# Two-layer attention block: wide score maxima, value sums in a score bank and later scaling in layer 0; an early shared rotary tile and a halved last gate slice in layer 1

## The chip, the cores and the metric

The kernel runs on 1 core of one Trainium2 chip. The metric is the device time of one execution in microseconds. The kernel before took 1701.79 us (median of 3 runs, 1701.4 to 1703.03).

## The reference

Two layers act on 1024 latent tokens and 256 context tokens, each 1024 wide, in float32. In each layer the tokens are normalised and modulated, projected to queries, keys, values and a gate, go through softmax attention, are multiplied by silu(gate) and projected back:

```python
y = (o * silu(g)) @ w_out          # per layer
x = x + gate * y
# layer 0: 16 query heads of width 64, 4 key/value heads; latent queries read 1024 latent + 256 context keys,
#          context queries read the 256 context keys only
# layer 1: 16 heads; score = q_nope . k_nope (64 wide) + q_rope . k_rope (32 wide, one rotary key for all heads);
#          only latent queries
p = softmax(scale * q k^T);  o = p v
```

The result is the latent stream after both layers.

## The kernel before, in words

Products need float32 accuracy, so an operand is split into a high and a low part and a product is three matmuls: high x high, high x low, low x high.

**Attention** (class `Attention`, one object per layer) walks over units. A latent unit of layer 0 is one head with its 1024 queries; a context unit is the four heads of one key group with 4 x 256 queries. Layer 0 has 20 units in the order of `units`: latent heads 0 to 3, a context unit, heads 4 to 7, a context unit, heads 8 to 15, two context units. Layer 1 has 16 latent units. `run` (L640 onwards) goes through them: for each key tile of 128 keys (10 in a latent unit, 2 in a context unit of layer 0) `scores_by_halves` (L486) computes a score tile `st` of 128 keys by 1024 queries in two PSUM banks. The contraction is only 64 wide, so queries 0 to 511 work in rows 0 to 63 of the array and queries 512 to 1023 in rows 64 to 127, side by side: four pairs of matmuls in layer 0 (three products, and one that subtracts the query's maximum), five in layer 1. ScalarE takes the exp (L508) into `p`. After all key tiles of a unit follow, in this order:

- `run_turns`: for a unit whose maxima are complete, TensorE turns the 128x8 maxima (L422), VectorE casts them into `crow` (one buffer, L424), and two loads carry them into the row that the last score product subtracts (`shift`, a tile per unit in flight; `minus` holds the -1 that selects the row);
- `add_up`: GpSimd adds up the exp tiles (`acp`, L542), helped by VectorE for the last four (`pair_sum`, `acd`, L528);
- `totals` of the unit before: TensorE sums over the keys (L597) into a maxima bank, VectorE turns it and takes the reciprocal; `later` sets when the rows are spread (4 steps on), the output scaled by them on GpSimd (6) and stored (9);
- `do_av`: the value sums (L555) into the bank `av`, then ScalarE copies them out (L576) in `finish`.

The maxima of units ahead are computed between the scores (`max_parts`, L385): a half step is 128 queries by 512 keys in one PSUM bank `mx`, one matmul, and one reduction on VectorE (L395; L404 for context keys). Two half steps go with each key tile, one for each half of the array; `lead` says how many were done before the first unit, in layer 0 among the last gate slices (four at a time).

**PSUM** has eight banks. In layer 0's attention: three for `mx`, four for two score tiles, one for `av`.

**Order.** In `run` the instructions of TensorE, VectorE and ScalarE are issued in the order written; GpSimd and the load queue SP, and all engines in the gate slices and projections around it, are ordered by a planner. Each engine works in its order.

**Layer 1's start.** The last score product of layer 1 reads the shared tile `KS`: the rotary key and a row of -1, for all heads. It is opened in `l1_open_late` with the late tiles, in memory that the hidden state `hT` has until the last gate slice (L1728).

Of the kernel before, what the change touches and what calls it, by code (L numbers as in the profile page):

```python
# [19 lines left out]
P = 128  # L20
D = 1024
KT = D // P
# [6 lines left out]
HALVES = (True, True)  # L29

# [6 lines left out]
def hybrid_kernel(ctx: ExitStack, tc: tile.TileContext, ins: dict, out: bass.AP):  # L37
# [271 lines left out]
    class Attention:  # L309
# [15 lines left out]
        def open_early(self, st):  # L325

            l = self.l
            self.kp = st.enter_context(tc.tile_pool(name=f"kp{l}", bufs=self.ops["kbufs"], side="right", reuse_waits="tile"))
            self.qp = st.enter_context(tc.tile_pool(name=f"qp{l}", bufs=self.ops["qbufs"], side="right", reuse_waits="tile"))
            self.ps_m = st.enter_context(tc.tile_pool(name=f"psm{l}", bufs=3 if HALVES[l] else 2, space=PSUM, side="right", reuse_waits="tile"))  # L330
            if HALVES[l]:
                self.ops["open"](self, st)

        def open_late(self, st, stp):
            l = self.l
            self.op = st.enter_context(tc.tile_pool(name=f"op{l}", bufs=3 - l, reuse_waits="tile"))
            if l and HALVES[l]:
                self.ops["open_late"](self, stp)
# [71 lines left out]

        def do_shift(self, u):
# [8 lines left out]
            def turn():  # L420
                t = self.ps_m.tile([P, 512], F32, name="mx", tag="mx")[:8, :P]
# [11 lines left out]
        def start_unit(self):  # L433
# [3 lines left out]
            s["m"] = self.sm.tile([P, 8, 3 if lat else 1], F32, name="m", tag="m" if lat else "mc")  # L437
# [3 lines left out]
            if HALVES[self.l]:  # L441
# [9 lines left out]
        def next_maxima(self, upto, limit):  # L451

            steps = []
            while self.done < upto:
# [5 lines left out]
                self.done += 1  # L460
                half, parts = self.max_parts(u, m)
# [30 lines left out]
        def scores_by_halves(self, u, kt, p, steps):  # L492
# [11 lines left out]
            for half, parts in steps:  # L504
                at_ = (last + 2) // 2 if half and self.l else 0
# [25 lines left out]
        def add_up(self, u, parts, last):  # L531
# [3 lines left out]
            for b in parts:  # L535
# [5 lines left out]
                t = self.ap.tile([P, 1024], F32, name="acp", tag="acp", bufs=2) if len(held) == 2 else a  # L541
# [4 lines left out]
        def do_av(self, u, group, ps):  # L546
# [3 lines left out]
            if group[0] == kts[0]:  # L550
                s["av"] = self.ps_o.tile([P, 512], F32, name="av", tag="av")
# [19 lines left out]
        def finish(self, u):  # L571
# [21 lines left out]
            def total():  # L593
                t = s["av"] if u is not self.units[-1] and not HALVES[l] else self.ps_m.tile([P, 512], F32, name="mx", tag="mx")
# [9 lines left out]
                self.later((4, spread), (6, scale), (9, store))  # L604
# [24 lines left out]
        def run(self, lead, ahead, extra, tail):  # L629
# [3 lines left out]
            with tc.manual_schedule(engines={mybir.EngineType.PE, mybir.EngineType.DVE, mybir.EngineType.Activation}):  # L633
                for t, u in enumerate(self.units):
# [13 lines left out]
                    for group in (kts[:cut], kts[cut:]):  # L648
# [21 lines left out]
                        if final:  # L670
                            tail()
                        self.run_turns()
# [7 lines left out]
                        while self.totals:  # L680
                            self.totals.pop(0)()
# [5 lines left out]
                        self.step += (2 + len(group)) // 3  # L687
                while self.totals:
                    self.totals.pop(0)()
# [520 lines left out]
    def l0_open(at, st):  # L1210
        pool_ = st.enter_context(tc.tile_pool(name="shift0", bufs=1, **right))
        at.minus = pool_.tile([P, P], F32R, name="minus")
        at.shift = [pool_.tile([P, 512], F32R, name=f"shift{i}") for i in range(4)]
        for t in (at.minus, *at.shift):
            pool.memset(raw(t), 0.0)
        for n in range(2):
            pool.memset(raw(at.minus[64 * n:64 * n + 1, :]), -1.0)

    def l0_load_halves(u, at, lat, KH, KL):
# [3 lines left out]
        QH = qp.tile([P, 512], F32R, name="QH", tag="QA")  # L1223
        QL = qp.tile([P, 512], F32R, name="QL", tag="QB")
        for t, src in ((QH, q0h), (QL, q0l)):
            for n in range(2):
                dst = raw(t[64 * n:64 * n + 64, :])
                if lat:
                    h = u["h"]
                    sp.dma_start(dst, src[h // 2, 64 * (h % 2):64 * (h % 2) + 64, 512 * n:512 * n + 512])  # L1230
                else:
                    sp.dma_start(dst.rearrange("p (a n) -> p a n", a=2),
                                 src[2 * g:2 * g + 2, 64 * n:64 * n + 64, NL:].rearrange("a p n -> p a n"))
        X = at.shift[i]
        return dict(KH=KH, KL=KL, QH=QH, QL=QL, X=X, minus=at.minus, crow=[X[64 * n:64 * n + 1, :] for n in range(2)])
# [42 lines left out]
    def l0_maxima(s, n):  # L1278
        r = slice(64 * n, 64 * n + 64)
        return [(s["QH"][r, :], s["KH"][r, :])]  # L1280

    def l0_scores(s, kt, n=None):
        ks = slice(kt * P, (kt + 1) * P)
        if n is not None:
            r = slice(64 * n, 64 * n + 64)
            return [(s["KH"][r, ks], s["QH"][r, :]), (s["KL"][r, ks], s["QH"][r, :]),
# [16 lines left out]
    at = Attention(0, units, dict(scale=0.125, load=l0_load, scores=l0_scores, maxima=l0_maxima, mparts=1, open=l0_open, kbufs=2, qbufs=3, vw=256))  # L1303
# [21 lines left out]
    wo.append(load_weight(ins["l0_w_out"], KT, 512, 512, 0, todo=pieces))  # L1325
# [3 lines left out]
    at.run(28, 3, pieces, lambda: first.extend(fetch_first(0, 2)))  # L1329
# [269 lines left out]
    at = Attention(1, units, dict(scale=float(96 ** -0.5), load=l1_load, scores=l1_scores, maxima=l1_maxima, mparts=2, open=l1_open, open_late=l1_open_late,  # L1599
# [201 lines left out]
```

## Time and profile before

| | |
|---|---|
| median of 3 runs | 1701.79 us |
| the profiled execution | 1701.99 us, its span 1700.2 us |
| granted TensorE clock, mean | 0.996 |
| attention of layer 0, first score to last totals | 372.25 to 748.8 us |
| attention of layer 1, first score to last totals | 1189.42 to 1608 us |
| busy: TensorE / VectorE / ScalarE / GpSimd | 1659.7 / 1040.8 / 641.7 / 959.9 us |

Times in the views are microseconds from the start of the span. PE is TensorE's matmuls, PEld its weight loads, DVE VectorE, ACT ScalarE, POOL GpSimd, SP the load queue. In a line of the order of time stand start, duration, engine, line, operation, output<-inputs, shape and count; in brackets the idle time before it and what ended it. A line of stretches has the stretch, its length, the busy time of PE, PEld, DVE, ACT and POOL (with counts), then the granted TensorE clock (1.00 is full), the share of DMA engines busy and GB/s. A line of waits has who waited for whom: total, times, longest.

### The profile page before, as it was taken

The page shows a single profiled execution, that of the slowest core. Times are in us where ns is not written, and L with a number is a line of the kernel's source. Part 1 is how long each engine was busy: PE and PEld are TensorE (multiplying, and loading weights), DVE is VectorE, ACT ScalarE, POOL GpSimd, SP SyncE. Part 2 cuts the span into 40 slices and gives each one's busy share as a digit, 9 for nine tenths or more (in the row PEclk, how much of TensorE's full clock was granted, in tenths as well). Part 3 has the DMA queues.
Part 4 walks back from the last instruction along what each step waited for, and adds up shares of the span by engine and source line. Part 5 has one row for each costly group of instructions (what it writes and reads, how often), then busy time and mean ns, then how long its engine had stood idle before and what let it go on. Part 6 is the DMA issues. An engine that isn't in the chain of part 4 may idle for free. (4 is left out here: it accounts for less than half of the span.)

```text
span 1700.2 us, 27393 instructions
## 1 busy us (share of the span) xinstructions
PE 1659.7 (98%) x10212; PEld 1210.6 (71%) x10212; DVE 1040.8 (61%) x1807; ACT 641.7 (38%) x943; POOL 959.9 (56%) x646
## 2 busy tenths in 40 slices
PE   8999999999999999999989999999999999999998
PEld 5776768776566666557878889886766667667587
DVE  3765552357788777625675657754778777777231
ACT  4642212124455544432244533330434434344310
POOL 2673441218789988843245554450668787787521
PEclk9999999999999999999999999999999999999999
DMA  9547854521242422156433866776565555653451
GB/s 313 170 147 241 260 165 153 155 81 45 63 123 60 112 63 63 39 140 201 140 94 116 232 193 183 217 205 149 128 144 136 132 120 121 143 127 89 122 166 73
DMA packets 219821, 238.97 MB, mean 141 GB/s; under 512 B 23016, under 2 KB 159192, under 8 KB 219688
## 3 DMA queue, kind: packets, MB, share of 16 engines
q1 hardware_dynamic: 219264, 237.11, 50.0%
q8 instruction: 81, 1.33, 0.3%
q14 instruction: 52, 0.43, 0.1%
q10 hardware_dynamic: 424, 0.11, 0.0%
HBM read 163.37 MB, written 73.63 MB: 139 GB/s over the span
## 5 line engine op out<-in xcount | busy, mean ns | idle before, releaser
L395 DVE TENSOR_REDUCE m<-mx 128x1 f32<-128x512 f32 x512 | 333.5, 687 | 177.8 <-PE mx L393 174.2
L508 ACT ACTIVATE p<-st 128x1024 f32<-128x1024 f32 x328 | 335.9, 1027 | 164.2 <-PE st L501 144.1
L542 POOL TENSOR_TENSOR acp<-acp,p 128x1024 f32<-128x1024 f32 x128 | 305.3, 2385 | 7.8
L555 PE MATMUL av<-p,v 128*64 128x512 f32 x1312 | 291.2, 597 | 0.0
L555 PEld LDWEIGHTS av<-p,v 128*64 128x64 f32 x1312 | 91.1, 137 | 181.6 <-issue 179.0
L542 POOL TENSOR_TENSOR acp<-p 128x1024 f32<-128x1024 f32 x34 | 81.4, 2395 | 147.6 <-ACT p L508 147.5
L542 POOL TENSOR_TENSOR acp<-acp,acd 128x1024 f32<-128x1024 f32 x60 | 141.9, 2364 | 20.9 <-DVE acd L528 17.8
L528 DVE TENSOR_REDUCE acd<-p 128x512 f32<-128x1024 f32 x124 | 144.6, 1220 | 7.9 <-ACT p L508 7.8
L136 POOL TENSOR_TENSOR wb<-wraw,wa 128x512 fp32r<-128x512 f32 (+3 forms) x73 | 95.4, 1325 | 78.7 <-ACT wa L157 78.7
L93 PE MATMUL mm<-wa,hh 128*128 128x512 f32 (+2 forms) x336 | 127.5, 379 | 2.0 <-ACT hh L890 2.0
L501 PE MATMUL st<-QH,KH 64*128 64x512 f32 x320 | 122.6, 406 | 1.0 <-DVE gth L303 1.0
L95 PE MATMUL mm<-wa,hl 128*128 128x512 f32 (+2 forms) x336 | 121.5, 362 | 1.4 <-DVE hl L893 1.3
L94 PE MATMUL mm<-wb,hh 128*128 128x512 f32 (+2 forms) x336 | 121.0, 360 | 0.0
L501 PE MATMUL st<-QH,KL 64*128 64x512 f32 x320 | 119.4, 395 | 0.0
L576 ACT COPY os<-av 128x512 f32<-128x512 f32 x36 | 21.1, 587 | 260.2 <-PE av L555 206.8
L501 PE MATMUL st<-QL,KH 64*128 64x512 f32 x320 | 118.7, 392 | 0.0
L93 PE MATMUL y<-wa,oh 128*128 128x512 f32 (+1 forms) x296 | 114.1, 386 | 0.0
L95 PE MATMUL y<-wa,ol 128*128 128x512 f32 (+1 forms) x296 | 113.5, 383 | 0.0
L94 PE MATMUL y<-wb,oh 128*128 128x512 f32 (+1 forms) x296 | 113.5, 383 | 0.0
L404 DVE TENSOR_REDUCE m<-mx 128x2 f32<-128x512 f32 x144 | 94.2, 688 | 22.2 <-PE mx L403 18.8
L393 PE MATMUL mx<-KH,QH 64*128 64x512 f32 x256 | 102.8, 407 | 0.3 <-DVE m L404 0.3
L93 PE MATMUL mm<-hh,wa 128*128 128x512 f32 x256 | 101.9, 398 | 0.6 <-DVE qt L1675 0.6
(240 smaller groups left out, 3940.1 us busy)
## 6 DMA issues: line engine op xcount, KB each, us to landing
mraw<-in_l_w_mod SPq DMA_DIRECT2D x64, 256.0 KB
wraw<-in_l_w_in SPq DMA_DIRECT2D x28, 512.0 KB
KH<-k1h SPq DMA_DIRECT2D x32, 320.0 KB
KL<-k1l SPq DMA_DIRECT2D x32, 320.0 KB
rb<-rrow SPq DMA_DIRECT2D x72, 128.0 KB
mraw<-in_l_w_mod SPq DMA_DIRECT2D x16, 512.0 KB
sgd<-gth SPq DMA_DIRECT2D x32, 256.0 KB
wraw<-in_l_w_out SPq DMA_DIRECT2D x16, 512.0 KB
```

The lines of the kernel that those rows point to most:

```text
L93: pe.matmul(ps, lhsT=lh(k), rhs=rh(k), start=first and i == 0, stop=False)
L94: pe.matmul(ps, lhsT=lh(k), rhs=rl(k), start=False, stop=False)
L95: pe.matmul(ps, lhsT=ll(k), rhs=rh(k), start=False, stop=last and i == len(ks) - 1)
L136: eng.tensor_sub(lo, a, b)
L393: pe.matmul(held["m"][:, cs], lhsT=q[:, t * P:(t + 1) * P], rhs=k[:, ks], start=j == 0, stop=j == len(pairs) - 1)
L395: dve.reduce_max(s["m"][:, i, n:n + 1], held["m"], axis=AX.X)
L404: dve.reduce_max(s["m"][:, 2 * i:2 * i + 2, 2 if u["kind"] == "lat" else 0], m.rearrange("p (a b) -> p a b", a=2), axis=AX.X)
L501: pe.matmul(ps[:, n * 512:(n + 1) * 512], lhsT=lh, rhs=rh, start=j == 0, stop=j == last)
L508: act.activation(p, ps, AF.Exp, scale=self.ops["scale"])
L528: dve.reduce_sum(t[:, ns], p2.rearrange("p a n -> p n a")[:, ns, :], axis=AX.X)
L542: pool.tensor_add(t, a, b)
L555: pe.matmul(s["av"][64 * n:64 * n + 64, :], lhsT=s["v"][:, kt, u["vc"]:u["vc"] + 64], rhs=p[:, n * 512:(n + 1) * 512], start=kt == kts[0], ...
```

## The change

Layer 0:
- A maxima step is wide: 128 queries against all 1024 latent keys (keys 0 to 511 in rows 0 to 63, 512 to 1023 in rows 64 to 127), into a two-bank tile and with one reduction of 1024. For that all 1024 queries (`QA`) are loaded into both halves of the rows. Two such buffers take four banks. One wide step goes with each key tile; two at a time and at most 14 in all among the gate slices.
- The bank `av` is gone. The value sums go into a buffer of the score tiles, or, once no maxima are left to do, into a maxima buffer.
- Totals are no longer made in a context unit (but for the last two units); where two are made together, the second's later steps are three further on. Spreading, scaling and storing come 4, 8 and 11 steps on. `acp` has three buffers.
- One `shift` tile holds the rows of all units in flight, and `minus` has a selector for each.
- The low parts of the output weight are computed half on VectorE (share 2), not all on GpSimd.

Layer 1: `KS` is opened with the early tiles (`l1_open`). The last gate slice is computed as two slices of 256 columns.

```diff
-            self.ps_m = ... bufs=3 if HALVES[l] else 2 ...
+            self.ps_m = ... bufs=2 if WIDE[l] or not HALVES[l] else 3 ...
-            for name in (("ps_s", "ps_o"), ("ps_o", "ps_s"))[l]:
+            for name in (("ps_s",) if WIDE[l] else ("ps_s", "ps_o"), ("ps_o", "ps_s"))[l]:
+        def wide_max(self, u, step):
+            s = self.state[id(u)]
+            kind, i = step
+            held = {}
+            def part(n):
+                if n == 0:
+                    held["m"] = self.ps_m.tile([P, 1024], F32, name="mx", tag="mx")
+                m, (q, k) = held["m"], self.ops["maxima"](s, n)[0]
+                if kind == "lat":
+                    pe.matmul(m[:, n * 512:n * 512 + 512], lhsT=q[:, i * P:(i + 1) * P], rhs=k[:, n * 512:n * 512 + 512],
+                              start=True, stop=True)
+                else:
+                    for a in (2 * n, 2 * n + 1):
+                        t = 4 * i + a
+                        pe.matmul(m[:, a * 256:(a + 1) * 256], lhsT=q[:, t * P:(t + 1) * P], rhs=k[:, NL:NT], start=True, stop=True)
+                if n == 0:
+                    return
+                if kind == "lat":
+                    dve.reduce_max(s["m"][:, i, 0:1], m, axis=AX.X)
...
+        def av_tile(self, u):
+            pool_, tag = (self.ps_s, "st") if self.todo or self.started < len(self.units) else (self.ps_m, "mx")
+            t = pool_.tile([P, 1024], F32, name="avt", tag=tag)
+            self.state[id(u)]["av"] = t[:, :512]
...
-                t = self.ap.tile([P, 1024], F32, name="acp", tag="acp", bufs=2) if len(held) == 2 else a
+                t = self.ap.tile([P, 1024], F32, name="acp", tag="acp", bufs=3 - self.l) if len(held) == 2 else a
...
-                self.later((4, spread), (6, scale), (9, store))
+                self.later(*((d + gap, fn) for d, fn in zip(self.ops["gaps"], (spread, scale, store))))
...
-                                count += 2
+                                count += 1 if WIDE[self.l] else 2
+                        if WIDE[self.l] and group[0] == kts[0]:
+                            self.av_tile(u)
                         self.run_turns()
...
-                        while self.totals:
-                            self.totals.pop(0)()
+                        gap = 0
+                        while self.totals and (whole or late or final):
+                            self.totals.pop(0)(gap)
+                            gap += 3
...
-        at.minus = pool_.tile([P, P], F32R, name="minus")
-        at.shift = [pool_.tile([P, 512], F32R, name=f"shift{i}") for i in range(4)]
+        at.minus = pool_.tile([P, 4, P], F32R, name="minus")
+        at.shift = pool_.tile([P, 512], F32R, name="shift")
...
-        QH = qp.tile([P, 512], F32R, name="QH", tag="QA")
+        QA = qp.tile([P, NL], F32R, name="QA", tag="QA")
...
+                sp.dma_start(dst, q0h[h // 2, r, :NL])
...
-    wo = [load_weight(ins["l0_w_out"], KT, 0, 512, 0, todo=pieces)]
+    wo = [load_weight(ins["l0_w_out"], KT, 0, 512, 2, todo=pieces)]
-                    at.maxima(at.done + 4, 2)
+                    at.maxima(min(at.done + 2, 14), 2)
-    at.run(28, 3, pieces, lambda: first.extend(fetch_first(0, 2)))
+    at.run(14, 3, pieces, lambda: first.extend(fetch_first(0, 2)))
...
-    def l1_open_late(at, st):
-        at.KS = st.enter_context(tc.tile_pool(name="rope1s", bufs=1, reuse_waits="tile")).tile([P, NT], F32R, name="KS")
+        at.KS = st.enter_context(tc.tile_pool(name="rope1s", bufs=1, **right)).tile([P, NT], F32R, name="KS")
...
-            gate_slice(1, c, m, s0, 512, (wg, wg1)[c], hT, ps_mm, wkg)
+            for s1, n in ((s0, 256), (s0 + 256, 256)) if (c, m, s0) == todo_g[-1] else ((s0, 512),):
+                gate_slice(1, c, m, s1, n, (wg, wg1)[c], hT, ps_mm, wkg)
```

More of the change, by code (lines that the diff above doesn't have):

```diff
@@ L29 @@
 HALVES = (True, True)
+WIDE = (True, False)
 def raw(ap):
@@ L420, in turn @@
             def turn():
-                t = self.ps_m.tile([P, 512], F32, name="mx", tag="mx")[:8, :P]
+                if not WIDE[self.l]:
+                    t = self.ps_m.tile([P, 512], F32, name="mx", tag="mx")[:8, :P]
+                else:
+                    t = self.ps_m.tile([P, 1024], F32, name="mx", tag="mx")[:8, :P]
                 pe.transpose(t, m, ident)
@@ L440, in start_unit @@
                 s.pop("rest")()
-            if HALVES[self.l]:
+            if WIDE[self.l]:
+                if lat:
+                    self.todo += [(u, ("lat", i)) for i in range(8)]
+                self.todo += [(u, ("ctx", i)) for i in range(2)]
+            elif HALVES[self.l]:
                 if lat:
@@ L504, in scores_by_halves @@
             for half, parts in steps:
-                at_ = (last + 2) // 2 if half and self.l else 0
+                at_ = (last + 2) // 2 if half and not WIDE[self.l] else 0
                 streams[half][at_:at_] = parts
@@ L550, in do_av @@
             if group[0] == kts[0]:
-                s["av"] = self.ps_o.tile([P, 512], F32, name="av", tag="av")
+                if not WIDE[self.l]:
+                    s["av"] = self.ps_o.tile([P, 512], F32, name="av", tag="av")
                 s["v"] = self.load_v(u)
@@ L591, in finish, with total @@
             cr = sm.tile([P, 8], F32, name="cr", tag="cr")
-            def total():
-                t = s["av"] if u is not self.units[-1] and not HALVES[l] else self.ps_m.tile([P, 512], F32, name="mx", tag="mx")
+            def total(gap):
+                if WIDE[l]:
+                    t = self.ps_m.tile([P, 1024], F32, name="mx", tag="mx")[:, :512]
+                else:
+                    t = s["av"] if u is not self.units[-1] and not HALVES[l] else self.ps_m.tile([P, 512], F32, name="mx", tag="mx")
                 for i, part in enumerate(s["total"]):
@@ L687, in run @@
                         self.step += (2 + len(group)) // 3
+                gap = 0
                 while self.totals:
-                    self.totals.pop(0)()
+                    self.totals.pop(0)(gap)
+                    gap += 3
             self.run_deferred(self.step)
@@ L1222, in l0_load_halves @@
         qp = at.qp if i < 3 else at.qp2
-        QH = qp.tile([P, 512], F32R, name="QH", tag="QA")
+        QA = qp.tile([P, NL], F32R, name="QA", tag="QA")
         QL = qp.tile([P, 512], F32R, name="QL", tag="QB")
[L1225 to L1235, printed above, removed]
+        for n in range(2):
+            dst = raw(QA[64 * n:64 * n + 64, :])
+            low = raw(QL[64 * n:64 * n + 64, :])
+            if lat:
+                h = u["h"]
+                r = slice(64 * (h % 2), 64 * (h % 2) + 64)
+                sp.dma_start(dst, q0h[h // 2, r, :NL])
+                sp.dma_start(low, q0l[h // 2, r, 512 * n:512 * n + 512])
+            else:
+                for par in range(2):
+                    sp.dma_start(dst[:, 512 * par:512 * par + 512].rearrange("p (a n) -> p a n", a=2),
+                                 q0h[2 * g:2 * g + 2, 64 * par:64 * par + 64, NL:].rearrange("a p n -> p a n"))
+                sp.dma_start(low.rearrange("p (a n) -> p a n", a=2),
+                             q0l[2 * g:2 * g + 2, 64 * n:64 * n + 64, NL:].rearrange("a p n -> p a n"))
+        X = at.shift
+        return dict(KH=KH, KL=KL, QA=QA, QL=QL, X=X, minus=at.minus[:, i, :],
+                    crow=[X[64 * n + i:64 * n + i + 1, :] for n in range(2)])
     def l0_load(u, at):
@@ L1301, in hybrid_kernel @@
         units.insert(pos, ctxu[g])
-    at = Attention(0, units, dict(scale=0.125, load=l0_load, scores=l0_scores, maxima=l0_maxima, mparts=1, open=l0_open, kbufs=2, qbufs=3, vw=256))
+    at = Attention(0, units, dict(scale=0.125, load=l0_load, scores=l0_scores, maxima=l0_maxima, mparts=1, open=l0_open, gaps=(4, 8, 11), kbufs=2, qbufs=3, vw=256))
     stE = ExitStack()
@@ L1598, in hybrid_kernel @@
                               kts=list(range(TT))))
-    at = Attention(1, units, dict(scale=float(96 ** -0.5), load=l1_load, scores=l1_scores, maxima=l1_maxima, mparts=2, open=l1_open, open_late=l1_open_late,
+    at = Attention(1, units, dict(scale=float(96 ** -0.5), load=l1_load, scores=l1_scores, maxima=l1_maxima, mparts=2, open=l1_open, gaps=(4, 6, 9),
                                   kbufs=3, qbufs=3, vw=128))
```

30 lines of the change are left out of this document (19 added, 11 removed).

## The prediction, made before the result was known

> **What bounds the kernel now.** I read the page first, then the waits of TensorE, then the order of time around the places the diff touches.
>
> ```profile
> span 1700.2 us, 27393 instructions
> PE 1659.7 (98%) x10212; PEld 1210.6 (71%) x10212; DVE 1040.8 (61%) x1807; ACT 641.7 (38%) x943; POOL 959.9 (56%) x646
> ...
> L395 DVE TENSOR_REDUCE m<-mx 128x1 f32<-128x512 f32 x512 | 333.5, 687 | 177.8 <-PE mx L393 174.2
> L528 DVE TENSOR_REDUCE acd<-p 128x512 f32<-128x1024 f32 x124 | 144.6, 1220 | 7.9 <-ACT p L508 7.8
> ```
>
> TensorE is covered for 98% of the span, so a change can help only by removing its few idle gaps, or by removing slow stretches inside "busy": matmul ends are modelled, so a matmul that was held up still counts as busy. The waits name the gaps of this change:
>
> ```profile
> PE mx L597 <- POOL acp L542: 3.3, 2, 1.7
> PE st L501 <- DMA KS<-kr1h: 2.0, 1, 2.0
> PE st L501 <- DVE gth L303: 1.0, 1, 1.0
> ```
>
> These three are 6.3 us in all (total, times, longest). The rest has to be read from spacing. I number the 20 units of layer 0 by their place t: latent heads, with the context units at t=4, 9, 18 and 19.
>
> **Maxima among the gate slices of layer 0 (gain).** Nine times a group of four half maxima stands between the gate matmuls. One of them:
>
> ```profile
> 324.23 0.73 PE L393 MATMUL mx<-KA,QH 64*128 64x512 f32 x3
> 324.89 0.50 PE L93 MATMUL mm<-hh,wa 128*128 128x512 f32 x1
> 325.22 0.40 PE L94 MATMUL mm<-hl,wa 128*128 128x512 f32 x1
> 325.55 0.49 PE L393 MATMUL mx<-KA,QH 64*128 64x512 f32 x1
> 325.97 0.50 PE L95 MATMUL mm<-hh,wb 128*128 128x512 f32 x1
> 326.31 0.39 PE L93 MATMUL mm<-hh,wa 128*128 128x512 f32 x1
> ```
>
> Only three banks exist, so the fourth maximum comes later, and every change between 64-row and 128-row matmuls costs an interval of 0.33 instead of 0.23. With the first interval taken as 0.33 too, from the last gate matmul before to 326.31 are 2.41 us, where four plain gate intervals of 0.227 would be 0.91: 1.50 lost per group, 13.5 in nine. After the change there are seven groups (two wide maxima each, stopped at 14), and both wide buffers are free, so the four matmuls go as two pairs: 0.33 + 0.66 + 0.33 less two plain intervals = 0.87 each, 6.1 in seven. Gain 7.4. The maxima not done here move into the first four key tiles of unit 0, which now run without maxima at the pace of exp (1.10, two in 2.20 at 460.94 below) and then take 1.16 (below): 0.25 more, against about as much lag that unit 0 then loses as the others do. Nothing. Ends: if the order stays broken, 7 x 1.50 leaves a gain of 3.0; if a group costs only its two pairs plus one change (0.7), 8.6. I take 7.4, nearest to the row.
>
> **Score phase of the latent units (small gain).** Unit t=1:
>
> ```profile
> 393.24 0.50 PE L393 MATMUL mx<-KA,QH 64*128 64x512 f32 x2
> ...
> 404.17 0.66 PE L393 MATMUL mx<-KA,QH 64*128 64x512 f32 x2
> 405.88 0.64 PE L597 MATMUL mx<-acp,twos 128*32 128x256 f32 x8
> 406.45 8.80 PE L555 MATMUL av<-p,v 128*64 128x512 f32 x40
> ```
>
> VectorE and ACT beside it, and the spacing of layer 1, whose key tiles are seven pairs and run free:
>
> ```profile
> 393.77 4.88 DVE L395 TENSOR_REDUCE m<-mx 128x1 f32<-128x512 f32 x8 [4.29 <-PE mx L393]
> ```
>
> ```profile
> 393.35 0.59 ACT L576 COPY os<-av 128x512 f32<-128x512 f32 x1 [7.92 <-PE av L555]
> ```
>
> ```profile
> 1246.16 0.70 PE st L501 x6
> 1247.79 0.70 PE st L501 x6
> ```
>
> A pair is 1.63 / 7 = 0.233, so TensorE needs 1.16 for a key tile of five. Eight half reductions in a chain take 4.88, 0.61 each, 1.22 per key tile. VectorE sets the pace: nine key tiles take 404.17 - 393.24 = 10.93, where 0.1 + 9 x 1.164 = 10.58 would do. The matmul work is unchanged (one wide step is two matmuls, as two half steps were). For a wide reduction the trace has the 1024-element sum at 1.22 (row L528); in a chain 0.61 + 512 elements at (1.220 - 0.687)/512 = 1.14. That is below 1.16, so the lag of 0.35 goes. Something takes part of its place: with two buffers the totals (L597) take the buffer of the ninth key tile's maximum and wait for its whole reduction: 0.53 until it starts (393.24 to 393.77), 1.22, and 0.06 for the signal = 1.81 after that tile's start, against 405.88 - 404.17 = 1.71 now. Net 0.25 per unit; 13 units (t = 1 to 3, 5 to 8, 10 to 15 are latent and have maxima): 3.2. Ends: 0 if the totals slip by the same 0.35, and 5.9 (the 0.35 and another 0.1 of 1.71 each) if they don't wait at all.
>
> The value sums in a score bank cost nothing: the next unit's second score tile needs the ACT copy (0.59), which ends at 393.94, 0.7 after the next unit's first maximum (393.24), while that tile's scores start 0.1 + 1.16 + 0.23 = 1.5 after it. Without this cover of 0.8 it would be 0.6 per unit. The halving of the weight remainder puts one subtraction per odd unit on VectorE, which is idle for 4.3 of each value sum (the bracket above); a subtraction of this size next to POOL is bounded by the 1.22 of row L528. The doubled query loads, 256 KB more per unit, meet DMA engines that read 0.00 to 0.26 busy in the windows below. The one shift tile for all units makes the last product of a unit wait for every row that is on its way; each of them is issued ahead of a value sum of 8.7 (406.45 to the next unit), and a cast and its two loads take 2.8 (709.89 - 707.13 below). All nothing.
>
> **No totals in context units (gain).** Units t=4 and t=9:
>
> ```profile
> 459.39 0.50 PE L393 MATMUL mx<-KA,QH 64*128 64x512 f32 x2
> 460.94 2.20 ACT L508 ACTIVATE p<-st 128x1024 f32<-128x1024 f32 x2 [0.84 <-PE st L501]
> 464.17 1.94 PE L555 MATMUL av<-p,v 128*64 128x512 f32 x8
> 466.04 0.50 PE L393 MATMUL mx<-KA,QH 64*128 64x512 f32 x2
> ...
> 554.27 0.51 PE L393 MATMUL mx<-KA,QH 64*128 64x512 f32 x2
> 558.71 1.01 PE L597 MATMUL mx<-acp,twos 128*32 128x256 f32 x8 [1.74 <-POOL acp L542]
> 562.79 0.50 PE L393 MATMUL mx<-KA,QH 64*128 64x512 f32 x2
> ```
>
> ```profile
> 558.00:560.00 2.00, 1.29 (x10) 0.45 (x12) 0.24 (x1) 1.05 (x3) 1.92 (x3) 0.71 0.00 0
> 560.00:562.00 2.00, 2.00 (x6) 0.47 (x4) 0.43 (x2) 0.00 (x0) 2.00 (x2) 0.50 0.26 70
> ```
>
> They last 6.65 and 8.52. In the second the granted clock (the number before the DMA share) falls to half after the 1.74 gap: 2 x (0.29 + 0.50) = 1.6 us lost on top. With no totals the next thing late is the second exp: it ends 460.94 + 2.20 - 459.39 = 3.75 after the start, then half a value sum (0.97): 4.8. Gains 1.85 and 3.7, less two totals of 0.57 (405.88 to 406.45) moved into t=5 and t=10: 4.4. The later scaling (8 and 11 instead of 6 and 9 steps) lets POOL wait less for a row that TensorE never waits for: nothing.
>
> **Three turns at t=16 (a new wait, loss).** With a lead of 14 and one step per key tile, all 168 steps are done at the last key tile of t=16. Its three pending turns, the totals and, as nothing is left to do, also its value sums then all take a maxima buffer, of which there are two. The turns now:
>
> ```profile
> 707.13 0.28 DVE L424 CAST crow<-mx 8x128 fp32r<-8x128 f32 x1
> 709.89 0.28 DVE L424 CAST crow<-mx 8x128 fp32r<-8x128 f32 x1 [2.49 <-DMA shift<-crow]
> 712.54 0.28 DVE L424 CAST crow<-mx 8x128 fp32r<-8x128 f32 x1 [2.37 <-DMA shift<-crow]
> ...
> 708.12 8.80 PE L555 MATMUL av<-p,v 128*64 128x512 f32 x40
> ```
>
> Each cast waits until the one before has left its single row tile. Now three banks and an own value bank keep this off TensorE: the value sums start at 708.12. With two buffers the third turn needs the first cast, the totals the second, the value sums the third (712.54 + 0.28 = 712.82): 4.7 us later. TensorE in order stands still for about 2.5 and then 2.1 with the totals between; a 1.74 gap cost 1.6 of clock above, so I add 2.0 (between 0 and 3). Loss 6.7, ends 0 (if the buffers are granted otherwise) and 7.7. [...]
>
> **Layer 1 (gain).** The shared tile KS is opened with the other early tiles, so its loads no longer wait for the hidden state's memory.
>
> ```profile
> 1194.00:1196.00 2.00, 2.00 (x12) 1.69 (x10) 1.07 (x2) 0.59 (x1) 0.00 (x0) 0.50 1.11 276
> 1196.00:1198.00 2.00, 2.00 (x16) 1.65 (x14) 0.92 (x3) 1.02 (x1) 0.54 (x1) 0.72 1.15 290
> ```
>
> The 2.0 wait goes, and with it the half clock behind it: 2 x (0.50 + 0.28) = 1.6. The last slice in halves shortens the chain to its VectorE product by about 0.4 (half of two operations) and adds some 0.3 of matmuls: 0.1. What is left is the 1.0 wait for that product, too short for the clock. Gain 3.7; ends 0 (KS still late) and 4.6 (the 1.0 gone too).
>
> **Sum.** -7.4 - 3.2 - 4.4 + 6.7 - 3.7 = -12.0. The profiled execution took 1701.99 (1.8 outside its span), 0.2 above the median of 1701.79: 1690.0.
>
> **Rivals.**
> A. Unit 16 doesn't stall: the slots come free otherwise. For it: nothing in the trace shows value sums in that pool. Against: only two buffers, and the casts' rhythm is plain. 1690.0 - 6.7 = 1683.3.
> B. The gate groups stay broken at 1.50, because that stretch is ordered by the planner and not by hand: 4.4 less gain, 1694.4.
> C. Slower: the wide reduction is dearer than the sum of row L528 and paces TensorE. Place: the score phase of the 14 units with maxima. At two single reductions without overlap, 1.37, each unit lags 10 x (1.37 - 1.16) = 2.1 instead of 0.35: +1.75 x 14 = 24.5 instead of -3.2, 1717.7. It decides from the point where it eats the other 8.8: (8.8 / 14 + 0.35) / 10 + 1.16 = 1.26 per reduction in the chain. Against: 1.14 worked out above, and the same engine does 1024 elements in 1.22 unchained.
> D. The change doesn't do what it says in layer 1: KS is opened early, but its new place is freed late: 3.7 less gain, 1693.7.
>
> **How the numbers follow.** Forecast 0.47, A 0.15, B 0.20, D 0.10, C 0.08. A change under 0.2% (3.4 us) can't be told from none. Forecast, A, B and D are faster (0.92); of these I leave 0.06 to small losses adding up to no change, where gate gain, clock and lag all end at their bad bounds (3.0, 0 and 7.7: 1702.0 - 3.0 - 4.4 + 7.7 - 3.7 = 1698.6), and 0.01 to worse: faster 0.85, same 0.06, slower 0.09. The range reaches from below A (part of the 5.9 in the score phase) to those bad bounds: 1682 to 1699; outside lie C and the tails.
>
> **What would show it.** Gate groups: four maxima in one piece, no gate matmul inside. Score phase: wide reductions of about 1.22, key tiles 1.16 apart, totals 1.8 after the ninth tile's start. Context units: 4.8 long, no wait for acp, full clock. t=16: TensorE waits for two casts, value sums 5 us after the first. Layer 1: no wait for KS, full clock at its start. The forecast is wrong if the unit t=16 doesn't stall, or if a wait for a maximum appears in every unit.

## The result, and the profile after

The kernel after took 1690.45 us (median of 4 runs, 1688.67 to 1691.93) beside 1701.60 us for the kernel before in the same comparison (4 runs, 1698.5 to 1703.03): a ratio of 0.9933, 95% interval 0.9917 to 0.9949. The forecast of 1690.0 holds. The profiled execution took 1690.33 us with a span of 1688.5, so 11.7 us of span are gone. They did not go quite where the prediction put them.

The page of the kernel after, and its waits of TensorE (total, times, longest):

```profile
span 1688.5 us, 27283 instructions
...
L430 DVE TENSOR_REDUCE m<-mx 128x1 f32<-128x1024 f32 x128 | 150.4, 1220 | 68.3 <-PE mx L421 67.7
```

```profile
PE tp L1747 <- DVE tl L88: 4.5, 4, 1.5
PE mx L645 <- DVE m L430: 3.4, 11, 0.4
```

The waits for `acp`, `KS` and `gth` are gone. New are the totals' (L645) 3.4 us in 11 units behind the wide reductions and the two waits for `crow` at t=16 (2.58 and 1.47, in the brackets below). In the query projection of layer 1 one wait grew from 2.6 us (L1688, in the waits before) to 4.5, and another of 1.9 (for `qa_ms`, L1638 before) is gone.

The order of time after, at the borders of the parts. First layer 0: a gate group, the start of the attention, t=1, the two context units with the starts after them, t=16, and the first output product:

```profile
323.54 0.73 PE L421 MATMUL mx<-KA,QA 64*128 64x512 f32 x4
324.20 0.50 PE L94 MATMUL mm<-hh,wa 128*128 128x512 f32 x1
...
364.82 0.50 PE L421 MATMUL mx<-KA,QA 64*128 64x512 f32 x2
...
385.60 0.50 PE L421 MATMUL mx<-KA,QA 64*128 64x512 f32 x2
...
396.38 0.40 PE L421 MATMUL mx<-KA,QA 64*128 64x512 f32 x2
...
398.19 0.64 PE L645 MATMUL mx<-acp,twos 128*32 128x256 f32 x8 [0.29 <-DVE m L430]
...
451.59 0.50 PE L421 MATMUL mx<-KA,QA 64*128 64x512 f32 x2
456.28 0.50 PE L421 MATMUL mx<-KA,QA 64*128 64x512 f32 x2
...
544.84 0.51 PE L421 MATMUL mx<-KA,QA 64*128 64x512 f32 x2
549.55 0.50 PE L421 MATMUL mx<-KA,QA 64*128 64x512 f32 x2
...
681.34 0.50 PE L421 MATMUL mx<-KA,QA 64*128 64x512 f32 x2
696.90 1.08 PE L645 MATMUL mx<-acp,twos 128*32 128x256 f32 x8 [2.58 <-DVE crow L461]
699.45 10.61 PE L600 MATMUL avt<-p,v 128*64 128x512 f32 x40 [1.47 <-DVE crow L461]
709.99 0.50 PE L545 MATMUL st<-QA,KA 64*128 64x512 f32 x2
...
741.92 0.50 PE L94 MATMUL y<-wa,oh 128*128 128x512 f32 x1
```

Then layer 1's first maxima and first value sums, after:

```profile
1143.09 0.50 PE L392 MATMUL mx<-KH,QH 64*128 64x512 f32 x2
...
1198.00 1.51 PE L600 MATMUL av<-p,v 128*64 128x512 f32 x6
```

The borders of the kernel before that were not shown yet:

```profile
372.25 0.50 PE L501 MATMUL st<-QH,KA 64*128 64x512 f32 x2
...
694.38 0.50 PE L393 MATMUL mx<-KA,QH 64*128 64x512 f32 x2
716.86 0.50 PE L501 MATMUL st<-QH,KA 64*128 64x512 f32 x2
...
748.80 0.50 PE L93 MATMUL y<-wa,oh 128*128 128x512 f32 x1
...
1149.67 0.69 PE L393 MATMUL mx<-KH,QH 64*128 64x512 f32 x2
...
1189.42 0.50 PE L501 MATMUL st<-QH,KH 64*128 64x512 f32 x1 [0.98 <-DVE gth L303]
...
1209.90 1.51 PE L555 MATMUL av<-p,v 128*64 128x512 f32 x6
```

Subtracting border from border gives the ledger. Every row is after less before:

| part | predicted | in the traces |
|---|---|---|
| up to the attention of layer 0 (372.25 to 364.82) | -7.4 | -7.43 |
| unit t=0 (20.99 to 20.78) | 0 | -0.21 |
| 13 latent units, moved totals left out (285.97 to 286.34 - 1.14) | -3.2 | -0.77 |
| context units t=4 and t=9 (15.17 to 9.40), moved totals of 1.14 added | -4.4 | -4.63 |
| t=16 (22.48 to 28.65) | +6.7 | +6.17 |
| t=17 to 19 (31.94 to 31.93) | 0 | -0.01 |
| first output product to layer 1's first maxima (400.87 to 401.17) | 0 | +0.30 |
| layer 1's first maxima to first value sums (60.23 to 54.91) | -3.7 | -5.32 |
| the rest of the span (490.30 to 490.50) | 0 | +0.20 |
| sum | -12.0 | -11.7 |

Three of the five terms are met within 0.6 us. The score phase gave 2.4 us less than forecast and layer 1 gave 1.6 more; that these two misses largely cancel, so that the total is met to 0.3, is luck. How far one trace can be trusted is seen from other executions. Seven kernels, the one after among them, have the same order up to the attention: they begin it between 363.52 and 364.89 (mean 364.45). Four, the one before among them, have the other order: 371.06 to 372.61 (mean 372.02). So the first row is 7.6, with single executions about 1 us apart.

One row does not stand up to this comparison. Three other kernels, among the experiments below, leave t=9 as it was before. They wait for `acp` there for 1.40, 1.75 and 1.92 us (1.74 before), yet at full clock: t=9 takes 6.53, 6.88 and 7.03 us in them, where it took 8.52 in the trace before. The run of the halved gate slice, with the longest of these waits and totals of 0.64 behind it:

```profile
558.82 0.64 PE L597 MATMUL mx<-acp,twos 128*32 128x256 f32 x8 [1.92 <-POOL acp L542]
```

So 1.5 to 2 us of the 4.63 in the row of the context units belong to a half clock that this one execution had. The last section has another pair of executions that differ in this way.

### The profile page after: what moved, and what is told of

It is laid out like the page before. It is cut to its first block, busy times and chain, and to the rows that moved or that the text cites. A ratio compares the mean times of both kernels' runs of the same rounds, so it can differ in the third digit from the quotient of the medians.

```text
span 1688.5 us, 27283 instructions
## 1 busy us (share of the span) xinstructions
PE 1646.4 (98%) x10236; PEld 1192.4 (71%) x10236; DVE 1044.3 (62%) x1652; ACT 642.1 (38%) x944; POOL 952.3 (56%) x632
## 5 line engine op out<-in xcount | busy, mean ns | idle before, releaser
L394 DVE TENSOR_REDUCE m<-mx 128x1 f32<-128x512 f32 x256 | 176.1, 691 | 92.9 <-PE mx L392 87.7
L430 DVE TENSOR_REDUCE m<-mx 128x1 f32<-128x1024 f32 x128 | 150.4, 1220 | 68.3 <-PE mx L421 67.7
L600 PE MATMUL avt<-p,v 128*64 128x512 f32 x672 | 151.0, 601 | 1.6 <-DVE crow L461 1.5
L600 PE MATMUL av<-p,v 128*64 128x512 f32 x640 | 141.1, 595 | 0.0
L137 POOL TENSOR_TENSOR wb<-wraw,wa 128x512 fp32r<-128x512 f32 (+3 forms) x65 | 86.5, 1346 | 80.2 <-ACT wa L158 80.2
L600 PEld LDWEIGHTS avt<-p,v 128*64 128x64 f32 x672 | 46.6, 138 | 96.3 <-issue 85.2
L600 PEld LDWEIGHTS av<-p,v 128*64 128x64 f32 x640 | 44.5, 137 | 88.3 <-issue 87.6
L94 PE MATMUL mm<-hh,wa 128*128 128x512 f32 (+1 forms) x264 | 103.2, 391 | 0.2 <-DVE qt L1734 0.2
```

What stands on the lines that cost most here:

```text
L94: pe.matmul(ps, lhsT=lh(k), rhs=rh(k), start=first and i == 0, stop=False)
L137: eng.tensor_sub(lo, a, b)
L394: dve.reduce_max(s["m"][:, i, n:n + 1], held["m"], axis=AX.X)
L430: dve.reduce_max(s["m"][:, i, 0:1], m, axis=AX.X)
L600: pe.matmul(s["av"][64 * n:64 * n + 64, :], lhsT=s["v"][:, kt, u["vc"]:u["vc"] + 64], rhs=p[:, n * 512:(n + 1) * 512], start=kt == kts[0], ...
```

## The experiments

**Three row tiles at t=16.** The rows of three turns get a tile each:

```diff
-                r = self.sm.tile([8, P], F32R, name="crow", tag="crow", bufs=1)
+                self.turned = getattr(self, "turned", 0) + 1
+                own = self.l or self.turned % 3 == 1
+                r = (self.sm if own else self.ap).tile([8, P], F32R, name="crow", tag="crow", bufs=1 if own else 2)
```

> The kernel after, with three row tiles for the casts instead of one in layer 0's attention, nothing else. Theory (the single row tile makes the stall of unit t=16): no cast waits for the loads of the one before, the totals and the value sums of t=16 follow the score products at once, the granted clock there stays 1.00, unit t=16 falls from 28.65 us to 22.5 and the kernel from 1690.3 to about 1684.2. Rival 1 (the two maxima buffers alone make the stall, whatever the row tile): unit t=16 stays above 27 and the time at 1690. Rival 2 (the one shift tile for all units makes the next loads wait): the waits for the casts move to the first scores of t=17, and under 3 us are gained.

Measured: 1685.14 us (4 runs, 1684.12 to 1689.65), ratio to before 0.9904 (0.9876 to 0.9931). Unit t=16 in the order of time:

```profile
694.36 0.64 PE L647 MATMUL mx<-acp,twos 128*32 128x256 f32 x8 [0.28 <-DVE crow L463]
694.93 8.80 PE L602 MATMUL avt<-p,v 128*64 128x512 f32 x40
```

The unit takes 22.56 us (681.10 to 703.66), and its value sums 8.80 instead of 10.61. The buffers of the maxima are still two; what stalled TensorE was the one row tile behind them. For want of two more such tiles, 512 bytes a partition each, the change paid 6.1 us.

**The value sums of t=16 in a score bank.**

```diff
-            pool_, tag = (self.ps_s, "st") if self.todo or ...
+            pool_, tag = (self.ps_s, "st") if self.turns or self.todo or ...
```

> The kernel after, with the value sums of t=16 in a score bank instead of a maxima buffer; the single row tile stays. Theory: only the totals still wait for the second cast (2.58 us); the gap of 1.47 us ahead of the value sums goes. If one gap of 2.6 us is enough for the half clock, the loss of about 2.3 us by the clock stays and t=16 takes 28.65 - 1.5 = 27.2 us. If it takes both gaps within a few us for that, the clock stays full and t=16 takes 28.65 - 1.5 - 2.3 = 24.9 us. Rival: a score bank is freed late and the value sums wait for exp instead: 28 us or more, with a wait for ACT in the row of the value sums.

Measured: 1687.22 us (one run). The unit and the granted clock (the number before the last two) in stretches of 2 us:

```profile
696.68 1.03 PE L645 MATMUL mx<-acp,twos 128*32 128x256 f32 x8 [2.58 <-DVE crow L461]
697.64 10.06 PE L600 MATMUL avt<-p,v 128*64 128x512 f32 x40
```

```profile
696.00:698.00 2.00, 1.32 (x10) 0.48 (x12) 0.28 (x1) 0.00 (x0) 1.23 (x1) 0.70 0.00 1
698.00:700.00 2.00, 2.00 (x6) 0.47 (x4) 1.09 (x2) 0.00 (x0) 0.00 (x0) 0.50 0.00 1
700.00:702.00 2.00, 2.00 (x12) 0.60 (x10) 2.00 (x3) 0.00 (x0) 0.38 (x1) 0.95 0.01 2
```

The wait of 1.47 is gone and the unit takes 26.50 (681.13 to 707.63). One gap of 2.58 has the clock halved here, for 2 x (0.30 + 0.50 + 0.05) / 0.5 = 3.4 us. It costs (1.03 - 0.64) + (10.06 - 8.80) = 1.65 us beside the undisturbed durations of the run above; with the second gap it was (1.08 - 0.64) + (10.61 - 8.80) = 2.25. So the result lies between the two cases of the expectation: the second gap goes with a longer half clock, 2 x (0.43 + 0.50 + 0.50 + 0.28) / 0.5 = 6.8 us in the kernel after (0.57, 0.50, 0.50 and 0.72 in the same way from 696 to 704), worth 0.6 us, and it is not needed for one. That compares single executions.

**What paces the key tiles.** Three kernels leave work out. In the first, the wide maxima look at half of the keys:

```diff
-                    dve.reduce_max(s["m"][:, i, 0:1], m, axis=AX.X)
+                    dve.reduce_max(s["m"][:, i, 0:1], m[:, :512], axis=AX.X)
...
```

> The kernel after, with work left out: the wide maxima of layer 0's latent keys are taken over 512 of 1024 keys (the matmuls stay), and the factor in layer 0's exp is a tenth so that nothing overflows. Question: what paces nine key tiles of t=1 at 10.78 us where TensorE needs 10.45 to 10.58. Theory V (VectorE's wide reductions of 1.22 us): the nine tiles fall to 10.5 and the totals no longer wait, unit t=1 21.90 to about 21.3. Theory A (the two score tiles come back from ScalarE's exp a little late): the nine tiles stay at 10.75 to 10.8, the wait of the totals alone goes, unit t=1 21.90 to 21.6.

In the second, exp does half of the queries, and what reads `p` reads that half twice:

```diff
-            act.activation(p, ps, AF.Exp, scale=self.ops["scale"])
+            c = slice(0, 512) if WIDE[self.l] and len(u["kts"]) > 4 and u is not self.units[0] else slice(0, 1024)
+            act.activation(p[:, c], ps[:, c], AF.Exp, scale=self.ops["scale"])
...
```

> The kernel after, with work left out: in layer 0's latent units from t=1 on, exp is made for 512 of 1024 queries only, and sums, totals and value sums use these twice (same matmuls, same reductions). Theory V (VectorE paces the key tiles): nine tiles of t=1 stay at 10.78 us, unit t=1 at 21.9. Theory A (the exp of 1.05 us gives the score tiles back late): the longer interval after every second first score product (0.29 to 0.34 instead of 0.23) goes, nine tiles fall to 10.45 to 10.55 and unit t=1 to about 21.6.

The third has both edits:

> The kernel after, with the work of both earlier halved runs left out together in layer 0: the latent maxima are reduced over 512 of 1024 keys (factor in the exp a tenth), and exp is made for 512 of 1024 queries, which sums and value sums use twice. Halving the reductions alone took the wait of the totals (0.29) away and left nine key tiles at 10.79 us (unit t=1 21.54); halving exp alone took nine tiles to 10.41 and raised that wait to 0.47 (21.68). Theory (two limits one behind the other: exp's return of the score tiles sets the pace, the last wide reduction the totals): together nine tiles 10.41 and no wait for the totals, t=1 about 21.2. Rival (they are the same slack seen twice): not below 21.5.

The three took 1685.14, 1687.96 and 1678.39 us, one run each. The reading goes by the unit.

Unit t=1, the tenth key tile's maximum and the totals, with the reductions halved:

```profile
395.81 0.40 PE L421 MATMUL mx<-KA,QA 64*128 64x512 f32 x2
...
397.26 0.64 PE L645 MATMUL mx<-acp,twos 128*32 128x256 f32 x8
```

With exp halved:

```profile
395.89 0.39 PE L421 MATMUL mx<-KA,QA 64*128 64x512 f32 x2
...
397.86 0.64 PE L650 MATMUL mx<-acp,twos 128*32 128x256 f32 x8 [0.47 <-DVE m L430]
```

With both, the totals stand without a wait:

```profile
397.54 0.64 PE L650 MATMUL mx<-acp,twos 128*32 128x256 f32 x8
```

VectorE's first reductions in the run with exp halved:

```profile
386.02 4.66 DVE L430 TENSOR_REDUCE m<-mx 128x1 f32<-128x1024 f32 x4 [4.05 <-PE mx L421]
390.59 1.23 DVE L432 TENSOR_REDUCE m<-mx 128x4 f32<-128x1024 f32 x1
```

From the starts of the unit, of its tenth tile's maximum, of the totals and of the next unit (us):

| | nine key tiles | totals after the tenth's start | unit t=1 |
|---|---|---|---|
| after (385.60, 396.38, 398.19, 407.50) | 10.78 | 1.81 | 21.90 |
| half reductions (385.02, 395.81, 397.26, 406.56) | 10.79 | 1.45 | 21.54 |
| half exp (385.48, 395.89, 397.86, 407.16) | 10.41 | 1.97 | 21.68 |
| both (385.69, 396.10, 397.54, 406.84) | 10.41 | 1.44 | 21.15 |

For the kernel after, theory A holds and theory V falls. Halving VectorE's work leaves the pace of the key tiles alone; halving exp brings it to 10.41, which is 1.16 a tile. In the kernel after, this is how ScalarE and TensorE stand at the third tile of t=1:

```profile
387.15 2.09 ACT L552 ACTIVATE p<-st 128x1024 f32<-128x1024 f32 x2 [0.85 <-PE st L545]
```

```profile
388.23 0.50 PE L545 MATMUL st<-QA,KA 64*128 64x512 f32 x2
388.57 0.40 PE L545 MATMUL st<-QA,KB 64*128 64x512 f32 x2
```

There are two score tiles, so the third tile needs the first back. Its exp is through at about 387.15 + 2.09 / 2 = 388.2, just when TensorE wants to write (388.23); the interval behind is 0.34 instead of 0.23, and it is 0.29 to 0.34 at every second tile; with exp halved it is 0.23 throughout. The wait is too short to be listed as one. VectorE is the second limit, right behind: with exp halved it sets the totals (0.47 instead of 0.29), and only both together give 21.15.

**Layer 1, its two parts singly, on the kernel before.** First `KS` alone among the early tiles:

```diff
...
+        at.KS = st.enter_context(tc.tile_pool(name="rope1s", bufs=1, **right)).tile([P, NT], F32R, name="KS")
...
```

> The kernel before, with only the shared rotary tile of layer 1 opened with the early tiles. From the first maxima of layer 1 to its first value sums the kernel before takes 60.3 us, the kernel after 54.9. Theory of the prediction: the wait of 2.0 us for KS and the half clock behind it (1.6) go, the wait of 1.0 for the last gate product stays: 60.3 - 3.6 = 56.7. Rival 1 (the gate product's wait has the same cause, memory or loads of the late tiles): it goes too, 55.6 or less. Rival 2 (the early place comes free late): 60.

Then the halved slice alone:

```diff
-            gate_slice(1, c, m, s0, 512, (wg, wg1)[c], hT, ps_mm, wkg)
+            for s1, n in ((s0, 256), (s0 + 256, 256)) if (c, m, s0) == todo_g[-1] else ((s0, 512),):
+                gate_slice(1, c, m, s1, n, (wg, wg1)[c], hT, ps_mm, wkg)
```

> The kernel before, with only the last gate slice of layer 1 computed as two slices of 256 columns. Theory of the prediction: shortens the wait for the last gate product by 0.4 us and adds 0.3 us of matmuls, the wait for KS stays: first maxima to first value sums 60.3 to 60.2 us. Rival (the halved slice alone takes the wait of 1.0 away): no wait for gth, but KS is then waited for 1.0 longer, so still about 60.2 in all, with a KS wait near 3; the two parts are worth more together than singly.

The waits of the first scores of layer 1 with the early `KS`:

```profile
PE st L499 <- DVE gth L303: 1.0, 1, 1.0
```

With the halved slice:

```profile
PE st L501 <- DMA KS<-kr1h: 1.0, 1, 1.0
PE st L501 <- POOL KS L1528: 1.0, 1, 1.0
```

With the early `KS`, first maxima to first value sums take 56.57 (1147.72 to 1204.29; 60.23 before), as forecast to 0.1, and it keeps the wait for the gate product (1696.49 us, one run). The halved slice takes that wait away, and TensorE waits the same 2.0 for `KS`: 59.97 (1149.18 to 1209.15), a gain of 0.26 (1701.34 us, one run). Singly they are worth 3.66 + 0.26 = 3.9, together 5.32: taking the gate product's wait away is worth something only where `KS` is no longer late behind it.

**No totals in the early context units, alone, on the kernel before.**

```diff
-                t = self.ap.tile([P, 1024], F32, name="acp", tag="acp", bufs=2) if len(held) == 2 else a
+                t = self.ap.tile([P, 1024], F32, name="acp", tag="acp", bufs=3 - self.l) if len(held) == 2 else a
...
-                        while self.totals:
-                            self.totals.pop(0)()
+                        gap = 0
+                        while self.totals and (whole or late or final):
+                            self.totals.pop(0)(gap)
+                            gap += 3
```

> The kernel before, with only the totals taken out of the two early context units of layer 0 (three acp buffers, the second totals' later steps three on). Theory: t=4 from 6.65 to 4.7 us, t=9 from 8.52 to 4.7, the next units 0.4 to 0.6 longer for the moved totals: 4.6 to 5.0 us in all; no wait for acp, clock full in t=9. Rival (three banks of half maxima and the later scaling of the other version are needed for it): the acp wait moves into t=5 and t=10, and under 2 us are gained.

```profile
553.10 0.50 PE L393 MATMUL mx<-KA,QH 64*128 64x512 f32 x2
557.90 0.50 PE L393 MATMUL mx<-KA,QH 64*128 64x512 f32 x2
```

Shown is t=9 and the start after it, 4.80 us; t=4 takes 4.83 (459.71 to 464.54), the units after them 0.44 and 0.45 more: a gain of 4.65, and the first output product comes 4.35 earlier, at 744.45. The part needs nothing of the others. Beside the kernels whose t=9 ran at full clock (6.53 to 7.03) the gain is 2.7 to 3.2. The time of its one run (1699.39 beside 1699.86) shows little of it, which is within what single runs differ by.

**Three half maxima a group, on the kernel before.**

```diff
-                    at.maxima(at.done + 4, 2)
+                    at.maxima(at.done + 3, 2)
...
-    at.run(28, 3, pieces, lambda: first.extend(fetch_first(0, 2)))
+    at.run(27, 3, pieces, lambda: first.extend(fetch_first(0, 2)))
```

> The kernel before, with three half maxima instead of four in each of the nine groups among layer 0's gate slices (27 ahead instead of 28), so that a group needs no more than its three banks. Theory (the fourth maximum, for which no bank is free, breaks the group): each group runs in one piece and costs 0.9 us instead of 1.50, the first score product of layer 0's attention comes at 372.25 - 9 x 0.6 = 366.8 us. Rival (the planner mixes them with gate matmuls anyway): groups are still broken and it comes at 371.5 to 372.3.

```profile
322.92 0.73 PE L393 MATMUL mx<-KA,QH 64*128 64x512 f32 x3
...
366.30 0.40 PE L501 MATMUL st<-QH,KA 64*128 64x512 f32 x2
```

No group is broken, and the first score product comes at 366.30 instead of 372.25 (forecast 366.8). The nine half maxima that are no longer done here lengthen unit 0 a little: t=1 begins at 387.65 instead of 393.24, 5.6 earlier. A group of three costs 0.87, as much as one of two wide maxima. So it was the fourth maximum without a bank that cost: most of the first term is to be had on the kernel before with one figure. The run took 1692.28 us (one run). Its t=9 takes 6.88 at full clock, with a wait of 1.75 for `acp`; that is no effect of the edit, but the other course that this wait can take.

**Versions that go further.** With 12 maxima ahead instead of 14, only two turns fall into t=16:

```diff
-                    at.maxima(min(at.done + 2, 14), 2)
+                    at.maxima(min(at.done + 2, 12), 2)
...
-    at.run(14, 3, pieces, lambda: first.extend(fetch_first(0, 2)))
+    at.run(12, 3, pieces, lambda: first.extend(fetch_first(0, 2)))
```

> The kernel after, with 12 wide maxima instead of 14 ahead of layer 0's attention (six groups among the gate slices instead of seven), nothing else. Theory: one group less saves 0.87 us; the last maxima then end in t=17, so t=16 has two turns instead of three and its value sums go into a score bank. The totals then need only the first cast, no wait for crow over 0.3 us, clock full, t=16 22.5 us instead of 28.65: 1690.3 - 6.1 - 0.9 = 1683.3. Rival 1 (the stall moves with the last turn): t=17 is 3 to 6 us longer than its 12.7 and the time stays at 1687 to 1690. Rival 2 (two steps less lead is too little): a wait of the transposes for VectorE's last reduction in every unit, 0.2 to 0.6 us each, and the gain is under 3 us.

Measured: 1686.36 us (4 runs, 1684.76 to 1687.49), ratio 0.9908 (0.9895 to 0.9921). That is 3 us short of the theory. Unit t=16 takes 22.17 as expected, but t=1 22.01 instead of 21.90, t=17 13.24 instead of 12.68, and t=18 9.46 instead of 7.99, with a wait for the last turn's row:

```profile
718.80 0.67 PE L545 MATMUL st<-shift,minus 64*128 64x512 f32 x2 [1.01 <-DMA shift<-crow]
```

Part of the stall moved with the last turn, as rival 1 said, but to t=18, and far less of it than the 3 to 6 us named there. On top of it the first value sums ahead of the totals:

```diff
                         self.run_turns()
+                        head = 2 if WIDE[self.l] and whole and not cut else 0
+                        if head:
+                            self.do_av(u, group[:head], ps[:head])
...
-                        self.do_av(u, group, ps)
+                        self.do_av(u, group[head:], ps[head:])
```

> As the run with 12 ahead, and in layer 0's latent units the value sums of the first two key tiles (four matmuls, 0.86 us) stand between the turns and the totals. Theory: the totals, which in the kernel after wait 0.29 us in most units for the last wide reduction, come 0.86 later and wait no more, while TensorE has work meanwhile: unit t=1 21.90 to 21.6, 11 to 13 units, 3.2 to 3.8 us, so 1679.5 to 1680. Rival 1 (the value sums wait instead, because their score bank is only free when the exp of the ninth key tile is through): unit t=1 stays at 21.8 to 21.9, 1683. Rival 2 (the later totals make GpSimd or the pair sums late): waits for acp or p of over 0.5 us in some units, 1683 to 1685.

Measured: 1689.63 us (6 runs, 1686.35 to 1693.25), ratio 0.9927 (0.9913 to 0.9941). That is far from the 1679.5 to 1680 expected, and no faster than without this edit. The wait of the totals goes, t=1 takes 21.69 instead of 22.01, but t=18 grows to 12.15 (2.31 of wait for the same row), and the projections behind take 404.67 us in this trace where they took 400.42 in the run above. TensorE's instructions stand in the same order in both, and this part takes from 398.83 to 402.41 in the other kernels, so it is most likely a difference between executions. The same edit with three row tiles and 14 ahead:

> The kernel after, with three row tiles for the casts and the value sums of the first two key tiles ahead of the totals (14 wide maxima ahead, as in the kernel after). Theory: t=16 22.5 us as with three row tiles alone, and t=1 21.90 to 21.6 as with 12 ahead, where moving these value sums made it 21.69 instead of 22.01; some nine units, 2.7 us: 1685.1 - 2.7 = 1682.4. Rival (the run with 12 ahead and moved value sums lost 3.3 us against the one without them because later turns and totals cost more elsewhere, in the last units and in the projections): 1685 to 1689, and the layer-0 attention ends earlier by 2 us or more while the time does not follow.

Measured: 1682.91 us (5 runs, 1680.33 to 1685.13), ratio to before 0.9889 (0.9870 to 0.9907). In t=1 the tiles keep their pace (10.78), the value sums fill the wait, and the unit takes 21.68 (385.13 to 406.81). This is the fastest version here. By the times it cannot be told from three row tiles alone (the intervals overlap); in the traces its layer-0 attention is 2.1 us shorter, from the first maxima to the first output product (364.36 to 734.41, against 363.52 to 735.63).

## Why the prediction was right, and where not

1. *Gate groups*: right in size and mechanism. From the last gate matmul (323.22) to the second one behind it (324.53), a group costs 0.32 + 0.66 + 0.33 less two intervals, 0.86 where 0.87 was worked out. Rival B fell: no group is broken; and the run with three half maxima showed the missing bank as the cause.
2. *Score phase*: the failed step is "That is below 1.16, so the lag of 0.35 goes", drawn from "VectorE sets the pace". The prediction divided 4.88 by eight, found 0.61 a half reduction, and took the match with the tile's pace for a cause. Nine tiles take 10.78 in the kernel after, where it expected 10.58, and halving the reductions leaves them at 10.79. Its two figures for VectorE were right: in the run with half exp four wide reductions in a chain take 390.59 - 386.02 = 4.57, 1.14 each, as worked out, and the totals come 1.81 after the start of the tenth tile (the prediction calls it the ninth), as said. But it never costed the return of a score tile: four products of 0.23 and their end, the exp of 1.03, and TensorE's next write, against 2 x 1.16 for two tiles. In the kernel after this is the limit, 0.04 a tile. What paced the kernel before was not tested. The term measured 0.77 instead of 3.2, between its low end and the value taken.

   A duration and a spacing differ in these traces: each wide reduction lasts 1.22 (the row of L430), and in the chain one takes 1.14. That is why rival C did not come; it does not find the pacing engine.
3. *Context units*: right in mechanism, with no wait for `acp`, and 4.69 and 4.71 us against 4.8 (its own sum, 3.75 + 0.97, is 4.72). The size was met by luck: the 1.6 of half clock that it read in t=9 belongs to that execution, and three kernels with the same unit and a like wait do without it. Against their t=9 the term is 2.6 to 3.1, not 4.4.
4. *Unit t=16*: right. Two casts are waited for, 2.58 and 1.47 us, where about 2.5 and 2.1 were expected. The clock cost 2.25, for which 2.0 stood. In the trace it is at half before the wait of 2.58 has ended (0.65 from 696 to 697, where the wait ends at 696.90) and still after the wait of 1.47 (0.50 from 700 to 702). Rival A fell: the unit stalls, and without the single row tile it does not.
5. *Layer 1*: the `KS` part was right to 0.1 (3.66 against 3.6). The step that failed is "what is left is the 1.0 wait for that product": the shortened chain was given 0.4, and the halved slice took the whole wait. (That this wait costs no clock agrees with the trace before: it ends at 1189.42, and the clock reads 1.00 from 1188 to 1192.) The term measured 5.32 where its upper end was 4.6. The halved slice adds 1.7 to the early `KS` (56.57 to 54.91), 0.7 above the wait that it removes. The traces show where the rest lies: with the early `KS` alone a half maximum of 0.50 stands by itself ahead of that wait (at 1186.18), which in the kernel after goes beside the first scores (at 1181.24), and the last gate matmul begins 0.2 later, counted from the first maxima (38.15 against 37.94). Why the planner orders them so is not shown. Rival D fell with the wait for `KS`.

The projections between the layers were taken as unchanged, and on the whole they were: +0.30, with one wait longer by 1.9 and another of 1.9 gone.

## What to carry to other kernels

A pace that equals one engine's chain is no proof that this engine sets it: cost the round of every buffer that the loop reuses (written, read, written again), and where two come within a few per cent, expect to gain only when both shrink. When a change takes banks or buffers together into fewer and larger ones, count at each border of a phase who asks for them and what each holder waits for itself; here a single row tile cost 6 us. Two waits of one engine, one behind the other, were worth more together here than singly, so test the parts both ways. And before a half clock or a wait in one trace goes into a sum, look whether other executions of the same order have it.

## What was not expected of the hardware

The length of an idle gap alone does not tell whether the clock is halved. The two runs with 12 maxima ahead have the same two gaps of TensorE in the key projection, 1.70 and 0.80 us in one and 1.92 and 0.80 in the other, with the same instructions in the same order. Without the moved value sums, and below it the granted clock (the number before the last two) in stretches of 2 us:

```profile
966.58 0.63 PE L1567 MATMUL tp<-ident,kn 128*128 128x128 f32 x4 [1.70 <-DVE kn L1531]
```

```profile
965.00:967.00 2.00, 0.42 (x5) 0.45 (x5) 0.69 (x1) 1.41 (x3) 2.00 (x2) 1.00 1.03 309
967.00:969.00 2.00, 1.21 (x8) 0.98 (x6) 1.66 (x3) 1.73 (x3) 1.05 (x2) 0.72 0.86 252
969.00:971.00 2.00, 2.00 (x9) 2.00 (x8) 1.90 (x2) 0.69 (x1) 2.00 (x2) 0.50 0.69 187
971.00:973.00 2.00, 2.00 (x12) 2.00 (x12) 0.75 (x1) 0.00 (x0) 1.60 (x1) 0.93 1.03 247
```

With them:

```profile
970.20 0.63 PE L1570 MATMUL tp<-ident,kn 128*128 128x128 f32 x4 [1.92 <-DVE kn L1534]
```

```profile
967.00:969.00 2.00, 1.28 (x10) 0.93 (x8) 1.27 (x4) 1.17 (x2) 1.31 (x1) 1.00 1.00 280
969.00:971.00 2.00, 0.80 (x5) 0.58 (x5) 0.73 (x2) 1.55 (x3) 1.93 (x2) 1.00 1.05 316
971.00:973.00 2.00, 1.20 (x9) 1.23 (x10) 2.00 (x4) 1.53 (x3) 1.13 (x1) 1.00 0.68 191
973.00:975.00 2.00, 2.00 (x13) 2.00 (x12) 1.53 (x1) 0.49 (x1) 2.00 (x2) 1.00 0.89 245
```

With the shorter gaps the clock is at half for 2 x (0.28 + 0.50 + 0.07) / 0.5 = 3.4 us, with the longer ones it stays at 1.00. From the second group of transposes to the ninth matmul behind it pass 3.30 us in the first run (968.18 to 971.48) and 1.88 in the second (971.80 to 973.68): 1.4 us for the same work.

The same goes for t=9: the trace before has a half clock behind a gap of 1.74, where the totals take 1.01 us, while the run of the halved gate slice has a gap of 1.92 and no half clock, and its totals take 0.64. So in these runs a gap of this size has no fixed price, and executions of the same order of work differ by it. What decides between the two was not shown: no experiment here moved a gap on purpose.
